# Routed experts of a decoder trunk: the gather of an expert's rows in three steps, and the return of the rows half an expert later

## The chip, the cores and the metric

The kernel runs on one core of a Trainium2 chip. The metric is the device time of one execution in microseconds (us). A core has a matrix engine (PE, with its weight loads, PEld, beside it), a vector engine (DVE), a scalar engine (ACT), GpSimd (POOL) and SyncE (SP), each with a queue of its own that it works off in order; in this kernel SP issues all transfers (DMAs) from memory.

## The reference, cut to what matters

Two decoder layers on 256 tokens of width 1024. The second layer's channel mixer, which the change touches, sends each token through two of eight experts. An expert is a SwiGLU with a hidden width of 3584, so its weights are three matrices of 1024 x 3584 in 32-bit floats, 44 MB for one expert.

```python
def moe_swiglu(x, w_router, w_gate, w_up, w_down):
    ...
    logits = (xf @ w_router).astype(jnp.float32)
    top_logit, top_e = lax.top_k(logits, TOP_K)
    gate = jax.nn.softmax(top_logit, axis=-1)
    ...
        return swiglu(xb, w_gate[e], w_up[e], w_down[e])
    ...
    out = jnp.zeros((n_tok, D), jnp.float32).at[tok_buf].add(y.astype(jnp.float32) * g_buf[:, None])

def swiglu(h, wg, wu, wd):
    return (jax.nn.silu(h @ wg) * (h @ wu)) @ wd
```

## The kernel before, in words

**Split numbers.** Every 32-bit operand is split in two parts of a shorter format, `hi` and `lo`: ACT copies the tile to `hi` with rounding, DVE subtracts to get `lo` (`split`, line 117). A product is then two or three matmuls that add up in one bank of PSUM, the matrix engine's output memory.

**Weight tiles.** All experts' weights come in tiles of 128 x 2048 numbers (1024 KB), 42 for one expert: 14 of the gate matrix, 14 of the up matrix, 14 of the down matrix. For each tile SP issues one DMA (line 114), ACT makes `hi` and DVE makes `lo` (both recorded under line 119). `Tiles.next` (line 886) issues loads and splits for two tiles beyond the one that PE is to take (`AHEAD = 2`). In the trace the raw tiles are called `raw` or `xh`, their high parts `hi` or `xl`, their low parts `lo` or `lnp`, by the buffer that each happens to use.

**Even and odd experts.** The experts are put in an order so that those with many tokens stand at even places and those with few at odd places. An even place is a `Many` (up to 128 rows, three matmuls for a product, lines 137 to 139, 12 matmuls of 512 columns for a tile); an odd place is a `Few` (up to 64 rows, whose high and low parts lie side by side as 128 columns, two matmuls for a product, lines 930 and 931, 8 matmuls for a tile, and a small matmul with `pair`, line 949, that adds the two halves). The text says Many and Few for the two kinds, and e0 to e7 for the experts in order.

**Chunks.** An expert is four chunks: 1024, 1024, 1024 and 512 of its 3584 hidden columns. `run_chunks` (line 961) runs them in a software pipeline over all experts: the gate tiles of a chunk, then the transposes (`turn`) of the chunk before, then the up tiles of this chunk, then the down tiles of the chunk before, then `fold`. So an expert's last down tiles come after the gate and up tiles of the next expert's first chunk.

**Into and out of an expert.** `gather` (line 1154) makes one-hot matrices `oh` of the next expert's slots on DVE (line 1159), multiplies the tokens by them on PE (line 1169, in 32-bit floats), splits the result into that expert's rows, and transposes the one-hots to `ohT` (PE line 1176, DVE copy line 1178). All of it stands in the program ahead of the gate tiles of an expert's third chunk (`before` of chunk 2), for the next expert. At the end of the last chunk's down tiles, `finish` (line 1280) takes the sums: `take` splits them into `yh` and `yl`; then `give` returns the rows to the tokens' order with `ohT` on PE (line 1277, 4 matmuls for one block of 128 tokens) and adds them, weighted, to the running output `f` on DVE (line 1278, 2 instructions for one block); both blocks for e0 to e6, one block for e7.

**What sets the order.** A scheduler at build time gives each engine's queue its order, from the order of the program and from what it reckons to be ready. `tc.issue_after(x)` puts what is inside behind `x` on the engine of `x`, with no wait of its own. `Tiles.paced` (line 894) uses it twice: ACT's instructions inside go behind the `hi` of the last tile made so far, DVE's behind the `lo` of the last but one. Reading the gate sums, the up sums, `turn`, `fold` and `finish` are paced in that way; `gather` is not. In `finish` the return stands, besides, behind the last DVE instruction of `take`.

**PSUM.** Two sets of four banks: `m` (gate and up sums, transposes, gathered rows) and `a` (an expert's two sums of the down product, and the returned rows).

Of the kernel before, what the change touches and what calls it, by code (L numbers as in the profile page):

```python
# [16 lines left out]
DEPTH, T, D, P = 2, 256, 1024, 128  # L17
NB = T // P
# [3 lines left out]
D_FFN, D_EXP, N_EXP, PLE = 2816, 3584, 8, 256  # L22
FEW = 64
# [16 lines left out]
def tile_decoder_trunk(  # L40
# [48 lines left out]
    def mbank(shape, dt=F32):  # L89
        return psum.tile(shape, dt, name="m", tag="m", bufs=4)  # L90
# [26 lines left out]
    def split(hi, lo, src, eng=nc.vector):  # L117

        return nc.scalar.copy(hi, src).ins, eng.tensor_sub(lo, src, hi.bitcast(F32)).ins  # L119
# [46 lines left out]
    for b in range(NB):  # L166
        t = x_tile()
# [13 lines left out]
    before = const.tile([P, P], BF16, name="before", tag="before")  # L181
# [78 lines left out]
    def of_block(xs, b):  # L260
        return tuple(t[:, :, b, :] for t in xs)
# [29 lines left out]
    def load_ln(g, bb, i):  # L291
        t = act.tile([P, 2, D], F32, name="lnp", tag="lnp", bufs=1)
        nc.sync.dma_start(t[:, 0, :], dram(g, i * D, [[0, P], [1, D]]))
        nc.sync.dma_start(t[:, 1, :], dram(bb, i * D, [[0, P], [1, D]]))
        return t
# [531 lines left out]
    class Chunk:  # L827


        def __init__(self, x, ws, c0, n, acc, before=None, after=None):  # L830
            self.x_of, self.ws, self.c0, self.n, self.acc_of = x, ws, c0, n, acc
            self.before, self.after = before, after

        def parts(self, kind):

            if kind < 2:
# [2 lines left out]
                                  self.ws()[2][:, r:r + 256, :].rearrange("o (k p) n -> p (o k) n", p=P))]  # L839
                    for r in range(self.c0, self.c0 + self.n, 256)]  # L840

        def columns(self, kind):

            ps = [mbank([P, 512]) for _ in range(self.n // 512)]
            nk = 2048 // self.n
            for g in range(KD // nk):
                w = self.tiles.next()
                for n, t in enumerate(ps):
                    for k in range(nk):
                        s = slice(self.n * k + 512 * n, self.n * k + 512 * n + 512)  # L850
                        self.mm(t, self.x, nk * g + k, w, s, g + k == 0, nk * g + k == KD - 1)
            return ps

        def gate(self):
            if self.before:
                self.before()
            self.x = self.x_of()
            ps = self.columns(0)
            with self.tiles.paced():
                self.have_gate(ps)  # L860
# [6 lines left out]
        def down(self):  # L867
            acc = self.acc_of()
            for g in range(self.n // 256):
                r = self.c0 + 256 * g  # L870
                w = self.tiles.next()
                for k in range(2):
                    for n in range(2):
                        s = slice(D * k + 512 * n, D * k + 512 * n + 512)
                        self.mm(acc[n], self.ht, 2 * g + k, w, s, r + k == 0, r + 256 == D_EXP and k == 1)
            if self.after:
                with self.tiles.paced():
                    self.after()

    class Tiles:  # L880

# [79 lines left out]
    def run_chunks(chunks, made):  # L961
        parts = []
        for prev, ch in zip([None, *chunks], [*chunks, None]):
            parts += [*(ch.parts(0) + ch.parts(1) if ch else []), *(prev.parts(2) if prev else [])]
        tiles = Tiles(parts, made)
        for prev, ch in zip([None, *chunks], [*chunks, None]):
            if ch:
                ch.tiles = tiles
                ch.gate()
            if prev:  # L970
                with tiles.paced():
                    prev.turn()
            if ch:
                ch.up()
            if prev:
                prev.down()
            if ch:
                with tiles.paced():
                    ch.fold()
# [124 lines left out]
    def moe_ple(i, xt):  # L1104
# [10 lines left out]
        slot = mt([P, NB, N_EXP], "slot")  # L1115
        for b in range(NB):
# [7 lines left out]
            t = mbank([P, N_EXP])  # L1124
# [3 lines left out]
        for b in range(NB):  # L1128
# [12 lines left out]
            t = mbank([P, N_EXP])  # L1141
# [8 lines left out]
        def few(e):  # L1150

            return e % 2 == 1

        def gather(e, slots):

            oh = mt([P, NB, P], "oh", bufs=2)
            n = FEW if few(e) else P
            for b in range(NB):
                phase["picked"] = nc.vector.tensor_scalar(
                    oh[:, b, :].rearrange("p (s n) -> p s n", n=n), slot_i[:, None, :n].to_broadcast([P, P // n, n]),  # L1160
                    slots[:, b, e:e + 1], None, op0=OP.is_equal).ins
            xh, xl = of_block(xe, e % 2)
            ts = [mbank([P, 4, n]) for _ in range(2)]
            for b in range(NB):
                for g, t in enumerate(ts):
                    for k in range(4):

                        c = (4 * g + k) * P
                        nc.tensor.matmul(t[:, k, :], xt[b][:, c:c + P], oh[:, b, :n], start=(b + k == 0),  # L1169
                                         stop=(b == NB - 1 and k == 3))  # L1170
            for g, t in enumerate(ts):
                s = slice(4 * g, 4 * g + 4)
                phase["gathered"] = split(*((xh[:, s, :FEW], xh[:, s, FEW:]) if few(e) else (xh[:, s], xl[:, s])), t)
            t = mbank([P, NB, P])
            for b in range(NB):
                nc.tensor.transpose(t[:, b, :], oh[:, b, :], ident)
            ohT = mt([P, NB, P], "ohT", F32R, bufs=2)
            nc.vector.tensor_copy(ohT, t)
            return xh, xl, ohT


        with tc.issue_after(routed.ins):
            state = {0: gather(0, slot)}
        picked, gathered = phase["picked"], phase["gathered"]
        pp = ple_pre(i, abank, turned)

# [18 lines left out]
        t = mbank([P, N_EXP])  # L1205
# [25 lines left out]
        place = mt([P, N_EXP // 2, 2], "place")  # L1231
# [16 lines left out]
        slots = mt([P, NB, N_EXP], "slots")  # L1248
# [6 lines left out]
        f = []  # L1255
        for b in range(NB):
            t = x_tile()
# [4 lines left out]
        def take(e, acc):  # L1262

            yh, yl, _ = state[e]
            for n in range(2):
                s = slice(4 * n, 4 * n + 4)
                last = split(yh[:, s], yl[:, s], acc[n].rearrange("p (k n) -> p k n", n=P))[1]
            return last

        def give(e, b):  # L1270

            yh, yl, ohT = state[e]
            for n in range(2):
                s = slice(512 * n, 512 * n + 512)
                t = abank([P, 512])
                for k, y in enumerate((yh, yl)):
                    nc.tensor.matmul(t, ohT[:, b, :], y[:, 4 * n:4 * n + 4], start=(k == 0), stop=(k == 1))
                nc.vector.scalar_tensor_tensor(f[b][:, s], t, Gs[:, b, e:e + 1], f[b][:, s], op0=OP.mult, op1=OP.add)

        def finish(e, acc):  # L1280
            with tc.issue_after(take(e, acc)):
                give(e, 0)
                if e < N_EXP - 1:
                    give(e, 1)
                    state.pop(e)

        chunks, cols = [], [(0, 1024), (1024, 1024), (2048, 1024), (3072, 512)]
        for e in range(N_EXP):
            acc, ws = [], []

            def weights(e=e, ws=ws):

                if not ws:
                    if e == 0:
                        k = 0
                        ws.extend(w[0:1] for w in (wg, wu, wd))
                    else:
                        k = nc.values_load(which_i[0:1, e:e + 1], engines=[mybir.EngineType.SP], min_val=0, max_val=N_EXP - 1)
                        ws.extend(w[bass.ds(k, 1)] for w in (wg, wu, wd))
                return ws  # L1300

            def sums(acc=acc):
                if not acc:
                    acc.extend(abank([P, 512]) for _ in range(2))
                return acc

            for c, (c0, n) in enumerate(cols):
                chunks.append((Few if few(e) else Many)(
                    lambda e=e: state[e][0] if few(e) else state[e][:2], weights, c0, n, sums,
                    before=(lambda e=e: state.update({e + 1: gather(e + 1, slots)})) if c == 2 and e + 1 < N_EXP else None,  # L1310
                    after=(lambda e=e, acc=acc: finish(e, acc)) if c == len(cols) - 1 else None))

        made = []
        for g, load in enumerate(chunks[0].parts(0)):
# [6 lines left out]
        phase["hi"] = [x_T("xl", F32R).rearrange("p k b n -> p (k b n)")]  # L1321
        phase["lo"] = [act.tile([P, 2048], F32R, name="lnp", tag="lnp", bufs=1)]
        run_chunks(chunks, made)
        lnp2 = load_ln(ln2_g, ln2_b, i)

        def embed(b, xs, xps, tiles, lnp):
# [64 lines left out]
                for _ in ple[b]:  # L1391
                    pass

        tail(lnp2, lambda: give(N_EXP - 1, 1))


        full = nc.values_load(most_i[0:1, 0:1], min_val=0, max_val=T + P)
        with tc.If(full > P):
            for more in range(2):
                with tc.For_i(0, N_EXP, 1) as e:  # L1400
# [14 lines left out]
                    for g in range(2):  # L1415
                        t = mbank([P, 4, P])
# [104 lines left out]
```

## Time and profile before

| What | Before |
|---|---|
| median of 3 runs | 1484.36 us (1484.25 to 1484.56) |
| the profiled execution's own time | 1485.4 us |
| its span in the trace | 1483.6 us |
| PE, PEld busy | 1418.9 us (96%), 1165.1 us (79%) |
| DVE busy | 1207.4 us (81%) |
| ACT busy | 985.7 us (66%) |
| moved from memory | 436.31 MB, mean 295 GB/s |

The experts run from about 505 to 1445 us of the span. Matmuls overlap in the pipeline and their ends are modelled: a 512-column matmul is shown as some 0.39 us long, while the next one can start 0.23 us after it. So PE's busy share doesn't tell how near it is to its peak; the distance between starts does. The small groups of the profile are cut from its page.

### The profile page before, as it was taken

The numbers are of one execution on the slowest core, as the hardware profiler recorded it, in microseconds if no ns is written. First come the engines' busy times: TensorE is split into PE (matmuls) and PEld (weight loads), VectorE is DVE, ScalarE is ACT, GpSimd is POOL, SyncE is SP. The second block draws the span as 40 slices with busy tenths as digits, with TensorE's granted clock in tenths as the row PEclk, the third lists the DMA queues.
The fourth block names the chain that finished last, engine by engine and source line by source line (L and its number), as shares of the span: only waits on it lengthen the run. The fifth ranks groups of instructions, "written<-read, shape, count | busy, mean of one in ns | idle before, by whom it ended". The sixth has DMA issues, their size and how long they took to land.

```text
span 1483.6 us, 19473 instructions
## 1 busy us (share of the span) xinstructions
PE 1418.9 (96%) x7239; PEld 1165.1 (79%) x7239; DVE 1207.4 (81%) x1393; ACT 985.7 (66%) x1022; POOL 23.3 (2%) x34
## 2 busy tenths in 40 slices
PE   8999999999999999999999999999999999999966
PEld 7987888877987788877778877778887777887745
DVE  6867545467677897889998899988898998889987
ACT  6646433444755776678876777876687886777861
POOL 1000000001000000000000000000000000000000
PEclk9999999999999999999999999999999999999988
DMA  9533555535642499999999999999999999999971
GB/s 296 201 130 121 192 193 175 199 121 165 220 147 110 148 384 334 352 375 380 419 382 340 365 387 374 415 397 341 378 387 358 408 421 364 333 387 373 416 283 59
DMA packets 157382, 438.71 MB, mean 296 GB/s; under 512 B 19744, under 2 KB 41056, under 8 KB 157280
## 3 DMA queue, kind: packets, MB, share of 16 engines
q1 hardware_dynamic: 157280, 437.39, 78.8%
q8 instruction: 59, 0.97, 0.3%
q14 instruction: 43, 0.35, 0.1%
HBM read 436.31 MB, written 1.05 MB: 295 GB/s over the span
## 4 chain that ended last, share of the span: by engine, by line
PE 74%; DVE 13%; DMA 5%; issue 5%; ACT 2%; POOL 0%; SPq 0%; DVEq 0%; ACTq 0%; POOLq 0%
PE m L139 9%; PE m L137 9%; PE m L138 9%; PE a L137 9%; PE a L138 9%; PE a L139 9%; DVE lo L119 7%; PE m L931 4%; PE m L930 4%; DMA raw<-in_moe_w_down_dram 2%; PE m L596 2%; DVE lnp L119 2%; PE m L1169 2%; PE m L949 1%; DMA raw<-in_moe_w_up_dram 1%
## 5 line engine op out<-in xcount | busy, mean ns | idle before, releaser
L119 DVE TENSOR_TENSOR lo<-raw,hi 128x2048 fp32r<-128x2048 f32 (+1 forms) x287 | 640.1, 2256 | 96.5 <-PE m L139 37.7
L119 ACT CAST hi<-raw 128x2048 fp32r<-128x2048 f32 (+1 forms) x289 | 539.6, 1890 | 151.6 <-PE m L138 50.8
L137 PE MATMUL m<-hi,xh 128*128 128x512 f32 x540 | 212.5, 394 | 0.7 <-DVE xl L119 0.7
L139 PE MATMUL m<-lo,xh 128*128 128x512 f32 x540 | 206.8, 392 | 4.6 <-DVE lo L119 4.6
L138 PE MATMUL m<-hi,xl 128*128 128x512 f32 x540 | 210.5, 390 | 0.0
L931 PE MATMUL m<-lo,xh 128*128 128x512 f32 x356 | 136.0, 412 | 10.0 <-DVE lo L119 9.8
L930 PE MATMUL m<-hi,xh 128*128 128x512 f32 x356 | 131.6, 400 | 0.0
L119 DVE TENSOR_TENSOR lnp<-raw,xl 128x2048 fp32r<-128x2048 f32 x56 | 127.9, 2284 | 2.9 <-ACT xl L119 2.8
L139 PEld LDWEIGHTS m<-lo,xh 128*128 128x128 f32 x540 | 101.3, 188 | 26.6 <-DVE lo L119 5.3
L137 PEld LDWEIGHTS m<-hi,xh 128*128 128x128 f32 x540 | 101.4, 188 | 21.4 <-DVE xl L119 0.8
L138 PEld LDWEIGHTS m<-hi,xl 128*128 128x128 f32 x540 | 101.5, 188 | 20.8
L119 ACT CAST xl<-raw 128x2048 fp32r<-128x2048 f32 x56 | 107.3, 1916 | 12.0 <-DMA raw<-in_moe_w_gate_dram 4.0
L137 PE MATMUL a<-hi,hh 128*128 128x512 f32 x272 | 106.8, 395 | 1.6 <-ACT hh L119 1.6
L119 DVE TENSOR_TENSOR lo<-xh,hi 128x2048 fp32r<-128x2048 f32 x45 | 102.8, 2285 | 5.6 <-ACT hi L119 5.1
L138 PE MATMUL a<-hi,hl 128*128 128x512 f32 x272 | 107.0, 393 | 0.0
L139 PE MATMUL a<-lo,hh 128*128 128x512 f32 x272 | 102.5, 395 | 0.0
L931 PEld LDWEIGHTS m<-lo,xh 128*128 128x128 f32 x356 | 68.4, 192 | 30.1 <-DVE lo L119 16.6
L119 ACT CAST hi<-xh 128x2048 fp32r<-128x2048 f32 x45 | 86.3, 1918 | 3.0 <-DMA xh<-in_moe_w_gate_dram 0.9
L930 PEld LDWEIGHTS m<-hi,xh 128*128 128x128 f32 x356 | 68.9, 194 | 13.4
L137 PE MATMUL a<-hi,xh 128*128 128x512 f32 (+1 forms) x168 | 67.2, 406 | 7.1 <-DVE ls L613 3.1
L931 PE MATMUL a<-lo,hh 128*128 128x512 f32 x172 | 65.4, 420 | 6.2 <-DVE lo L119 4.8
L138 PE MATMUL a<-hi,xl 128*128 128x512 f32 (+1 forms) x168 | 67.1, 400 | 1.3 <-DVE xl L119 1.2
(354 smaller groups left out, 2382.5 us busy)
## 6 DMA issues: line engine op xcount, KB each, us to landing
raw<-in_moe_w_gate_dram SPq DMA_DIRECT2D x103, 1024.0 KB, 8.0
raw<-in_moe_w_up_dram SPq DMA_DIRECT2D x95, 1024.0 KB, 8.1
raw<-in_moe_w_down_dram SPq DMA_DIRECT2D x81, 1024.0 KB, 7.6
xh<-in_moe_w_down_dram SPq DMA_DIRECT2D x31, 1024.0 KB, 7.9
xh<-in_moe_w_up_dram SPq DMA_DIRECT2D x17, 1024.0 KB, 8.1
raw<-in_ffn_w_down_dram SPq DMA_DIRECT2D x11, 1024.0 KB, 4.8
raw<-in_w_in_dram SPq DMA_DIRECT2D x10, 1024.0 KB, 6.6
raw<-in_ffn_w_gate_dram SPq DMA_DIRECT2D x10, 1024.0 KB, 5.1
```

The costliest lines, as they stand in the source:

```text
L119: return nc.scalar.copy(hi, src).ins, eng.tensor_sub(lo, src, hi.bitcast(F32)).ins
L137: nc.tensor.matmul(o, lh, rh, start=start, stop=False)
L138: nc.tensor.matmul(o, ll, rh, start=False, stop=False)
L139: nc.tensor.matmul(o, lh, rl, start=False, stop=stop)
L596: nc.tensor.matmul(s[:, a, :], lhsT, rhs, start=True, stop=True)
L930: nc.tensor.matmul(o, x[:, k, :], w[0][:, s], start=start, stop=False)
L931: nc.tensor.matmul(o, x[:, k, :], w[1][:, s], start=False, stop=stop)
L949: nc.tensor.matmul(t[:, j, :], hs[j // 4][:, j % 4 * P:j % 4 * P + P], pair, start=True, stop=True)
L1169: nc.tensor.matmul(t[:, k, :], xt[b][:, c:c + P], oh[:, b, :n], start=(b + k == 0), stop=(b == NB - 1 and k == 3))
```

## The change

`Chunk` no longer has one function before its gate tiles and one after its down tiles. It has a table `hooks` of functions by place: a place is `(kind, g)`, ahead of the g-th tile of the gate (kind 0) or up (kind 1) tiles, or `"end"`, after the down tiles. Each function at a place runs inside `tiles.paced()`.

`gather` is cut in three: `pick` makes the one-hots, `gather` multiplies and splits, `back` transposes the one-hots. In an expert's third chunk they stand ahead of gate tile 0, ahead of gate tile 2, and ahead of up tile 2. `give` is cut in two: `give` has the matmuls and holds the four results in PSUM, `add` has the DVE additions. `take` stays at the end of the last chunk's down tiles; `give` for both blocks stands ahead of gate tile 2 of the next expert's second chunk, and `add` for both ahead of up tile 0 of that chunk. For e7, whose next expert does not exist, `give` and `add` of block 0 follow the last chunk as before, now without `issue_after`, and those of block 1 stay in the tail.

```diff
-        def __init__(self, x, ws, c0, n, acc, before=None, after=None):
+        def __init__(self, x, ws, c0, n, acc, hooks):
...
+        def at(self, place):
+
+            for f in self.hooks.get(place, []):
+                with self.tiles.paced():
+                    f()
+
         def columns(self, kind):
 
             ps = [mbank([P, 512]) for _ in range(self.n // 512)]
             nk = 2048 // self.n
             for g in range(KD // nk):
+                self.at((kind, g))
                 w = self.tiles.next()
...
         def gate(self):
-            if self.before:
-                self.before()
...
-            if self.after:
-                with self.tiles.paced():
-                    self.after()
+            self.at("end")
...
         def give(e, b):
 
             yh, yl, ohT = state[e]
+            ts = []
             for n in range(2):
-                s = slice(512 * n, 512 * n + 512)
                 t = abank([P, 512])
                 for k, y in enumerate((yh, yl)):
                     nc.tensor.matmul(t, ohT[:, b, :], y[:, 4 * n:4 * n + 4], start=(k == 0), stop=(k == 1))
+                ts.append(t)
+            return ts
+
+        def add(e, b, ts):
+            for n, t in enumerate(ts):
+                s = slice(512 * n, 512 * n + 512)
                 nc.vector.scalar_tensor_tensor(f[b][:, s], t, Gs[:, b, e:e + 1], f[b][:, s], op0=OP.mult, op1=OP.add)
-
-        def finish(e, acc):
-            with tc.issue_after(take(e, acc)):
-                give(e, 0)
-                if e < N_EXP - 1:
-                    give(e, 1)
-                    state.pop(e)
...
+            hooks = {
+                (1, (0, 2)): lambda e=e: state.update(given=[give(e - 1, b) for b in range(NB)]) if e else None,
+                (1, (1, 0)): lambda e=e: [add(e - 1, b, ts) for b, ts in enumerate(state["given"])] if e else None,
+                (2, (0, 0)): lambda e=e: state.update({e + 1: [pick(e + 1, slots)]}) if e + 1 < N_EXP else None,
+                (2, (0, 2)): lambda e=e: state[e + 1].extend(gather(e + 1, state[e + 1][0])) if e + 1 < N_EXP else None,
+                (2, (1, 2)): lambda e=e: state[e + 1].append(back(state[e + 1].pop(0))) if e + 1 < N_EXP else None,
+                (len(cols) - 1, "end"): lambda e=e, acc=acc: take(e, acc),
+            }
             for c, (c0, n) in enumerate(cols):
                 chunks.append((Few if few(e) else Many)(
                     lambda e=e: state[e][0] if few(e) else state[e][:2], weights, c0, n, sums,
-                    before=(lambda e=e: state.update({e + 1: gather(e + 1, slots)})) if c == 2 and e + 1 < N_EXP else None,
-                    after=(lambda e=e, acc=acc: finish(e, acc)) if c == len(cols) - 1 else None))
+                    {at: [f] for (place, at), f in hooks.items() if place == c}))
...
         run_chunks(chunks, made)
+        add(N_EXP - 1, 0, give(N_EXP - 1, 0))
```

## Rows read from the trace of the kernel before

**Rows 1.** Stretch: length, busy us of PE, PEld, DVE, ACT, POOL; clock, DMA share, GB/s.

```profile
630.00:650.00 20.00, 20.00 (x105) 16.88 (x104) 15.99 (x10) 18.93 (x16) 0.00 (x0) 1.00 1.03 420
650.00:660.00 10.00, 7.23 (x25) 5.51 (x24) 9.86 (x8) 3.29 (x3) 0.00 (x0) 0.83 0.78 291
660.00:695.00 35.00, 33.71 (x180) 27.83 (x180) 32.42 (x22) 29.14 (x24) 0.00 (x0) 1.00 1.00 368
695.00:730.00 35.00, 34.07 (x156) 25.77 (x156) 34.65 (x18) 30.82 (x22) 0.00 (x0) 1.00 1.03 417
600.00:615.00 15.00, 15.00 (x71) 12.43 (x70) 10.18 (x7) 10.31 (x8) 0.00 (x0) 1.00 0.80 293
795.00:860.00 65.00, 65.00 (x305) 53.65 (x304) 56.51 (x35) 48.10 (x33) 0.00 (x0) 1.00 0.94 353
```

**Rows 2.** Waits in 505:1445: who for whom, us in total, times, longest.

```profile
DVE ohT L1178 <- PE m L1176: 20.7, 4, 5.4
...
DVE x L1278 <- PE a L1277: 16.4, 7, 2.8
```

**Rows 3.** Groups by line in 505:1445: count | busy us, mean ns | idle before.

```profile
L119 DVE TENSOR_TENSOR lo<-raw,hi 128x2048 fp32r<-128x2048 f32 x223 | 502.4, 2284 | 17.2 <-ACT hi L119 17.0
L119 ACT CAST hi<-raw 128x2048 fp32r<-128x2048 f32 x223 | 421.2, 1916 | 50.3 <-DMA raw<-in_moe_w_up_dram 15.8 <-DMA raw<-in_moe_w_gate_dram 13.7 <-DMA raw<-in_moe_w_down_dram 5.1
...
L1278 DVE SCALAR_TENSOR_TENSOR x<-a,Gs,x 128x512 f32<-128x512 f32 x30 | 20.7, 746 | 16.4 <-PE a L1277 16.4
...
L119 ACT CAST xh<-m 128x256 fp32r<-128x256 f32 (+1 forms) x15 | 7.1, 473 | 39.8 <-PE m L1169 39.8
...
L1178 DVE CAST ohT<-m 128x256 fp32r<-128x256 f32 x8 | 3.4, 423 | 21.0 <-PE m L1176 20.7
L1159 DVE TENSOR_SCALAR oh<-slot_i,slots 128x128 f32<-128x128 f32 x14 | 3.3, 276 | 0.0
```

**Rows 4.** DVE's timeline at the step from e0 to e1: start, length, instruction, [idle before].

```profile
646.06 1.28 DVE L119 TENSOR_TENSOR xl<-a,xh 128x512 fp32r<-128x512 f32 x2
650.14 2.75 DVE L1278 SCALAR_TENSOR_TENSOR x<-a,Gs,x 128x512 f32<-128x512 f32 x4 [2.80 <-PE a L1277]
652.80 4.48 DVE L119 TENSOR_TENSOR lo<-raw,hi 128x2048 fp32r<-128x2048 f32 x2
```

**Rows 5.** SP's timeline there: the DMA issues.

```profile
643.97 2.58 SPq L114 DMA_DIRECT2D raw<-in_moe_w_up_dram  x2
655.11 0.37 SPq L114 DMA_DIRECT2D raw<-in_moe_w_down_dram  x1
```

**Rows 6.** PE's timeline there.

```profile
651.30 0.39 PE L930 MATMUL m<-hi,xh 128*128 128x512 f32 x1
651.52 0.39 PE L931 MATMUL m<-lo,xh 128*128 128x512 f32 x1
...
655.14 0.50 PE L931 MATMUL m<-lo,xh 128*128 128x512 f32 x1 [2.77 <-DVE lo L119]
```

**Rows 7.** DVE's timeline at the step from e1 to e2.

```profile
759.51 1.28 DVE L119 TENSOR_TENSOR xl<-a,xh 128x512 fp32r<-128x512 f32 x2
762.53 2.75 DVE L1278 SCALAR_TENSOR_TENSOR x<-a,Gs,x 128x512 f32<-128x512 f32 x4 [1.73 <-PE a L1277]
```

**Rows 8.** PE's timeline there.

```profile
767.53 0.50 PE L139 MATMUL m<-lo,xh 128*128 128x512 f32 x1 [1.53 <-DVE lo L119]
```

**Rows 9.** DVE's timeline around the gather in e1, a Few.

```profile
670.46 0.69 DVE L119 TENSOR_TENSOR xl<-m,xh 128x512 fp32r<-128x512 f32 x1 [0.23 <-ACT xh L119]
672.26 2.29 DVE L119 TENSOR_TENSOR lo<-raw,hi 128x2048 fp32r<-128x2048 f32 x1 [1.11 <-ACT hi L119]
675.03 2.29 DVE L119 TENSOR_TENSOR lnp<-xh,xl 128x2048 fp32r<-128x2048 f32 x1 [0.48 <-ACT xl L119]
```

**Rows 10.** DVE's timeline at a paced transpose in e0, a Many.

```profile
605.79 1.29 DVE L119 TENSOR_TENSOR hl<-m,hh 128x512 fp32r<-128x512 f32 x2 [3.81 <-ACT hh L119]
608.09 2.29 DVE L119 TENSOR_TENSOR lo<-xh,hi 128x2048 fp32r<-128x2048 f32 x1 [1.01 <-ACT hi L119]
```

More of the change, by code (lines that the diff above doesn't have):

```diff
@@ L827, in tile_decoder_trunk @@
     class Chunk:
-        def __init__(self, x, ws, c0, n, acc, before=None, after=None):
+        def __init__(self, x, ws, c0, n, acc, hooks):
             self.x_of, self.ws, self.c0, self.n, self.acc_of = x, ws, c0, n, acc
-            self.before, self.after = before, after
+            self.hooks = hooks
         def parts(self, kind):
@@ L1152, in few, with pick @@
             return e % 2 == 1
-        def gather(e, slots):
+        def pick(e, slots):
             oh = mt([P, NB, P], "oh", bufs=2)
@@ L1161, in gather @@
                     slots[:, b, e:e + 1], None, op0=OP.is_equal).ins
+            return oh
+        def gather(e, oh):
+            n = FEW if few(e) else P
             xh, xl = of_block(xe, e % 2)
@@ L1173, in gather, with back @@
                 phase["gathered"] = split(*((xh[:, s, :FEW], xh[:, s, FEW:]) if few(e) else (xh[:, s], xl[:, s])), t)
+            return xh, xl
+        def back(oh):
             t = mbank([P, NB, P])
@@ L1178, in gather @@
             nc.vector.tensor_copy(ohT, t)
-            return xh, xl, ohT
+            return ohT
         with tc.issue_after(routed.ins):
-            state = {0: gather(0, slot)}
+            oh = pick(0, slot)
+            state = {0: [*gather(0, oh), back(oh)]}
         picked, gathered = phase["picked"], phase["gathered"]
@@ L1392, in tail @@
                     pass
-        tail(lnp2, lambda: give(N_EXP - 1, 1))
+        tail(lnp2, lambda: add(N_EXP - 1, 1, give(N_EXP - 1, 1)))
         full = nc.values_load(most_i[0:1, 0:1], min_val=0, max_val=T + P)
```

## The prediction

> **What bounds the kernel now.** I read the page for the engines' shares, then the waits of the expert stretch, then a table by stretches, and last the timelines at the places that the change touches. The shares alone say little: PE 96%, DVE 81%, DMA full. By stretch it is two regimes. In a Many, PE has work without a break: 65.00 of 65.00 us busy, with the transfers at 353 GB/s, below the 420 that the same queue reaches elsewhere [rows 1]. A tile costs it 12 matmuls whose starts lie 0.23 us apart [rows 6], 2.8 us; DVE needs 2.28 us for the tile's `lo` and ACT 1.92 for its `hi` [rows 3]. In a Few a tile is 8 matmuls, 1.8 us, so DVE and the transfers take over: from 660 to 695 us DVE is busy 32.42 of 35 us while 368 GB/s are moved, and from 695 to 730 it is 34.65 of 35 at 417 GB/s [rows 1]. There each microsecond in which DVE does nothing delays a `lo`, and with it both PE and the raw buffer for which the next DMA waits.
>
> The place to look at is the step from a Many to a Few. `take` ends at 647.3; then DVE waits 2.80 us for PE's return matmuls, adds for 2.75 us, and starts the next `lo` at 652.80 [rows 4]. SP issues nothing from some 646 until 655.11 [rows 5], so only 291 GB/s move from 650 to 660 [rows 1]; PE runs out of tiles and waits 2.77 us [rows 6], after which the clock of that stretch averages 0.83 [rows 1], that is, some 3.4 us of its 10 at the lower level of 1.2 GHz instead of 2.4. At the step from a Few to a Many it is the same in small: DVE waits 1.73 us [rows 7], PE 1.53 us [rows 8]. Over all experts the wait ahead of the additions is 16.4 us in 7 waits [rows 2]: four of 2.8 (Many to Few) and three of 1.7 (Few to Many).
>
> **The change, part by part.**
>
> *The return, cut in two.* The 8 matmuls and 4 additions for one expert stay as they are; no work goes. What goes is the wait between them. The matmuls are now 2 gate tiles behind `take`, 3.7 us of PE in a Few and 5.6 in a Many, so `yl` (ready at 647.3, about 3 us after the last down matmul) is there when PE comes to them. The additions stand 2 tiles behind the matmuls. When DVE reaches them it has just made the `lo` of the first up tile, so PE is at most those few tiles behind; if DVE has to wait there, it is because it is ahead, and PE has tiles in hand.
>
> At the step to a Few (four times) I count the whole 2.80 as gained, 11.2 us. It could be 0, if the transfers bound the Few anyway, or 2.80 and a part of the slow clock. For the whole: from 650 to 695 us, 7.4 us of transfer at 420 GB/s were missed ((129 x 10 + 52 x 35) / 420, [rows 1]), so the queue has room to take up 2.8. Against more: DVE, which stays the limit, is not sped up by PE's clock.
>
> At the step to a Many (three times) PE is the limit, so I count PE's gap and not DVE's: 3 x 1.53 = 4.6 us [rows 8]. Bounds: 0, if a gap opens elsewhere, and 1.73 each.
>
> *The additions at their new place.* 4 x 0.746 [rows 3], merged 2.75 us of DVE, in one block behind `turn`. In a Few, DVE is the limit both at the old place and at the new one: 0. In a Many, the cover is what PE has in hand: with two split tiles, 5.6 us, against 2.75 for the additions and 2.28 for the next `lo`, 5.0. I take 0. With only one tile in hand and the 1.29 of `turn` ahead of them [rows 10], it is 1.29 + 2.75 + 2.28 - 2.8 = 3.5 us each in e2, e4 and e6. What waits behind them is DVE's next `lo`, and for that PE and SP's next DMA.
>
> *The holding of banks.* `given` holds all four `a` banks over two gate tiles and until the additions are done. The next expert's sums need two of them only at its first down tile, four up tiles after the additions: 4 x 1.8 = 7.4 us in a Few against 2.75. Cost 0. The gathered rows now take the two `m` banks that the gate sums leave free. `turn` has to have one back: after the last gather matmul that is a cast and a subtraction, about 1.2 us, against two gate tiles, 3.7 us or more. Cost 0, unless the splits come late; then it falls under the next item.
>
> *The gather.* Same instructions: two one-hots of 0.276 us, the matmuls, four split instructions, one copy of 0.423 us [rows 3]. In a Many the gather makes ACT and DVE wait long now, up to 5.4 us at DVE [rows 2], and PE is not idle for any of it (795 to 860, [rows 1]): nothing to gain; I take 0. In a Few (e1, e3, e5) DVE's waits around it are 0.23, 1.11 and 0.48, 1.8 us [rows 9]. Behind splits and with the one-hots made two tiles earlier they might go, a gain of 5.4 in all; or ACT's cast stands at the head of its queue while PE works off the matmuls between two tiles, and they become longer. The nearest rows are the present waits; I take no change, 0, with both ends kept for the range.
>
> *Queues.* No DMA is added or moved, and SP's order stays; its issues come earlier only because buffers come free earlier. POOL has no part. The end of the program (e7's return and the tail) does the same work as before. The start, e0's own gather, too.
>
> **Sum.** 11.2 + 4.6 = 15.8 us. The profiled execution's own time is 1485.4 (span 1483.6 and 1.8 around it), 1.0 above the median of the runs, 1484.36. So 1469.6 for that execution and 1468.6 for the median.
>
> **The rivals.**
>
> *Bigger: the gather's waits in the Few experts go as well.* 15.8 + 3 x 1.8 = 21.2, so 1463.2. For it: the one-hots no longer share a place with the multiplication, and DVE's part is behind a `lo`. Against: ACT's cast still has to wait for PE's matmuls, and PE now gets them in one place.
>
> *The transfers bound the Few.* From 695 us on they run at 417, which is all that the queue gave anywhere (420 from 630 to 650, [rows 1]); if the earlier start only makes the queue full earlier and PE ends at the same time, the 11.2 goes and 4.6 stays: 1479.8. Against: the 7.4 us missed before 695. The Trainium skill (DMA: Bandwidth & Descriptors, "Where 436 GB/s comes from") puts the ceiling of the core's sixteen ports at 435 GB/s. By that page a Few's 44 MB cannot take less than about 101 us, an estimate from its figure, so such a bound is real; the trace's 420 agrees with it to 4%. What it leaves open is whether a Few has transfers in hand when it starts.
>
> *The waits move along with the additions.* DVE comes to them before PE has done the matmuls, at the limit of the buffers, and stands still as long as before, in the DVE-bound part: 0, so 1484.4. Against: two tiles now lie between matmuls and additions, where none lay before.
>
> *Slower: one tile in hand at the new queue heads.* Each paced block has ACT or DVE standing at the head of its queue until PE has come to the block's matmuls. What follows is fixed: two casts of 0.47, a `hi` of 1.92, a `lo` of 2.28 [rows 3], 5.15 us until PE gets a new tile. The pacing guarantees only one finished `lo` at that point. If it is one, PE loses 5.15 - 2.8 = 2.35 in each of four Many gathers, 5.15 - 1.85 = 3.3 in each of three Few gathers, and 3.5 at the additions of three Many: 9.4 + 9.9 + 10.5 = 29.8, less 15.8: 14.0 slower, 1498.4. It decides from the point where the `lo` of the second tile is queued behind the block instead of ahead of it. Against: the paced transposes in e0 made DVE wait 3.81 and 1.01 us [rows 10] and PE was busy 15.00 of 15.00 us around them [rows 1], so two tiles were in hand there.
>
> **How the numbers follow.** The forecast as summed: 0.53, own range 1463 to 1476 (the clock, and 0.5 to 1 us for each step). The bigger gain: 0.15, down to 1456 if the slow clock's 4 x 1.7 us comes back too. Transfers: 0.12. Waits that move along: 0.08. Slower: 0.12. A measurement of this kernel can tell 0.2%, 3 us, from no change. Faster than 1481.4 are the first three, 0.80; within, 0.08; slower, 0.12. The range 1456 to 1482 leaves the last two out, 0.20.
>
> **What would show it.** Right: no wait of DVE ahead of the additions at either step, or waits there at places where PE has no gap; at the step from e0 to e1 no gap of PE and a clock of 1.00; SP issuing every 2.2 us through that step instead of the hole of some 9 us; and the Few experts' first 45 us at about 375 GB/s instead of 351 ((291 x 10 + 368 x 35) / 45, [rows 1]). The additions stand in the second chunk, with a `lo` right ahead of them and right behind them. Wrong: PE gaps in the Many experts near the gather or behind `turn` (the slower case), the hole at SP moved by some four tiles to the additions' new place (the waits move along), or PE's gaps gone at the steps and new ones of the same size in the 40 us behind them, at 420 GB/s (the transfers).

## The result and the profile after

The changed kernel takes 1467.15 us (median of 4 runs, 1465.99 to 1467.34) against 1484.46 for the kernel before (4 runs beside it): a ratio of 0.9886, 95% interval 0.9872 to 0.9900, 17.3 us less. Forecast were 1468.6 us and a range of 1456 to 1482. The profiled execution took 1467.25 us, its span 1465.4, 18.2 less than the span before (the profiled execution of the kernel before was about 1 us above the median of its runs, so the spans differ by more than the medians).

The first view is the table by stretches of the changed kernel: stretch, length, busy time of PE, PEld, DVE, ACT and POOL with instruction counts, granted clock, DMA share, GB/s. It answers to [rows 1].

```profile
648.00:658.00 10.00, 10.00 (x49) 8.36 (x47) 10.00 (x8) 7.99 (x7) 0.00 (x0) 1.00 1.03 422
658.00:695.00 37.00, 35.17 (x186) 28.20 (x185) 35.03 (x25) 30.22 (x24) 0.00 (x0) 1.00 1.01 394
695.00:730.00 35.00, 34.03 (x155) 25.65 (x154) 34.76 (x18) 30.06 (x22) 0.00 (x0) 1.00 1.02 405
785.00:850.00 65.00, 65.00 (x311) 54.03 (x310) 54.11 (x34) 43.98 (x31) 0.00 (x0) 1.00 0.92 349
```

The ten microseconds at the step from e0 to e1 moved 291 GB/s before and move 422 now; PE is busy for all of them instead of 7.23, and the clock is 1.00 instead of 0.83. The Many stretch (last row) is as it was: PE without a break, at 349 GB/s. PE still has a gap in the Few, of 1.1 us behind the additions, in each of the four:

```profile
662.25 0.50 PE L934 MATMUL m<-lo,xh 128*128 128x512 f32 x1 [1.12 <-DVE lo L119]
```


DVE's timeline of the changed kernel at that step (start, length, instruction, [idle before]); line 1297 is the addition, 1278 before. It answers to [rows 4].

```profile
645.75 1.28 DVE L119 TENSOR_TENSOR xl<-a,xh 128x512 fp32r<-128x512 f32 x2
647.27 4.49 DVE L119 TENSOR_TENSOR lo<-raw,hi 128x2048 fp32r<-128x2048 f32 x2 [0.24 <-ACT hi L119]
651.68 2.29 DVE L119 TENSOR_TENSOR lo<-xh,hi 128x2048 fp32r<-128x2048 f32 x1
653.88 0.68 DVE L960 TENSOR_TENSOR hl<-hl,m 128x512 f32<-128x512 f32 x1
654.48 0.74 DVE L1297 SCALAR_TENSOR_TENSOR x<-a,Gs,x 128x512 f32<-128x512 f32 x1
655.14 2.28 DVE L119 TENSOR_TENSOR lnp<-raw,xl 128x2048 fp32r<-128x2048 f32 x1
657.34 0.68 DVE L119 TENSOR_TENSOR hh<-hl,hh 128x512 fp32r<-128x512 f32 x1
657.94 2.06 DVE L1297 SCALAR_TENSOR_TENSOR x<-a,Gs,x 128x512 f32<-128x512 f32 x3
659.92 8.88 DVE L119 TENSOR_TENSOR lo<-raw,hi 128x2048 fp32r<-128x2048 f32 x4
```

Behind the split of the sums (`xl<-a`) the next `lo` follows after 0.24 us, where 2.80 us of waiting and 2.75 of additions stood. The additions come three tiles later, one ahead of a `lo` and three behind it, and wait for nothing. A second wait has gone with the first. Before, PE came so late out of the hole that ACT stood 6.71 us ahead of its copies of the sums (line 937), and DVE had to wait for the `hi` behind them (ACT's and DVE's timelines of the kernel before):

```profile
659.67 0.59 ACT L937 COPY w<-m 128x512 f32<-128x512 f32 x1 [6.71 <-PE m L931]
662.93 2.29 DVE L119 TENSOR_TENSOR lo<-raw,hi 128x2048 fp32r<-128x2048 f32 x1 [0.65 <-ACT hi L119]
```

That wait of DVE was 0.65 us in e1, 0.60 in e3, 0.51 in e5 and 0.44 in e7; ACT's wait in e1 is 1.92 now. Over all experts the group of the additions says the same: its idle time was 16.4 us [rows 3] and is now

```profile
L1297 DVE SCALAR_TENSOR_TENSOR x<-a,Gs,x 128x512 f32<-128x512 f32 x32 | 22.5, 742 | 0.0
```

SP's timeline there, the answer to [rows 5]. The hole from 646 to 655 us is one from 646 to 649.6, and a smaller one follows: of the next issues one comes at 657.45 and the one behind it at 662.23, beside PE's gap.

```profile
643.65 2.58 SPq L114 DMA_DIRECT2D raw<-in_moe_w_up_dram  x2
649.59 2.57 SPq L114 DMA_DIRECT2D raw<-in_moe_w_down_dram  x2
```

The step from e1 to e2 on DVE, the answer to [rows 7]: the `lo` follows the split at once, and the additions wait for nothing.

```profile
755.75 1.28 DVE L119 TENSOR_TENSOR xl<-a,xh 128x512 fp32r<-128x512 f32 x2
756.95 2.28 DVE L119 TENSOR_TENSOR lo<-raw,hi 128x2048 fp32r<-128x2048 f32 x1
...
763.55 1.40 DVE L1297 SCALAR_TENSOR_TENSOR x<-a,Gs,x 128x512 f32<-128x512 f32 x2
```

Both kernels issue the same 336 weight transfers in the same order, so the issue of the same tile in both traces can be subtracted. That gives where the time comes from, step by step (issue after less issue before, in us, each read a little behind the step):

| | before the first step | e0 to e1 | e1 to e2 | e2 to e3 | e3 to e4 | e4 to e5 | e5 to e6 | e6 to e7, with e7 |
|---|---|---|---|---|---|---|---|---|
| lies earlier by | 0.3 | 3.7 | 5.6 | 8.9 | 10.7 | 13.5 | 15.3 | 19.3 |
| this step | | 3.4 | 1.9 | 3.3 | 1.8 | 2.8 | 1.8 | 4.0 |

Four steps from a Many to a Few give 13.5 us, three from a Few to a Many 5.5. The last two transfers lie only 18.3 earlier, and with them the end.

The length of an expert on DVE, from one split of the sums to the next, shows the same without the end. For e1, before and after (columns as in the table by stretches):

```profile
646.06:759.51 113.45, 107.81 (x510) 86.11 (x510) 105.14 (x64) 91.37 (x67) 0.00 (x0) 0.98 1.00 391
645.75:755.75 110.00, 106.56 (x510) 84.63 (x510) 104.77 (x65) 91.11 (x67) 0.00 (x0) 1.00 1.02 406
```

DVE does the same work in 3.45 us less. The other three Few experts are shorter by 3.30, 2.88 and 3.07, 12.7 in all, and the three Many that follow a Few by 1.83, 1.76 and 1.75, 5.3 in all.

### The profile page after: what moved, and what is told of

Its sections match the earlier page's. It is cut to its first block, busy times and chain, and to the rows that moved or that the text cites. A ratio compares the mean times of both kernels' runs of the same rounds, so it can differ in the third digit from the quotient of the medians.

```text
span 1465.4 us, 19472 instructions
## 1 busy us (share of the span) xinstructions
PE 1413.5 (96%) x7239; PEld 1161.0 (79%) x7239; DVE 1206.4 (82%) x1393; ACT 984.4 (67%) x1022; POOL 21.1 (1%) x34
## 4 chain that ended last, share of the span: by engine, by line
PE 69%; DVE 15%; issue 6%; DMA 5%; ACT 3%; SPq 1%; POOL 0%; DVEq 0%; ACTq 0%; POOLq 0%
PE a L137 9%; PE a L138 9%; PE a L139 9%; DVE lo L119 9%; PE m L137 8%; PE m L139 8%; PE m L138 8%; PE m L934 3%; PE m L933 3%; DVE lnp L119 2%; DMA raw<-in_moe_w_gate_dram 2%; DMA raw<-in_moe_w_up_dram 2%; PE m L596 2%; PE m L1177 2%; ACT hi L119 1%
## 5 line engine op out<-in xcount | busy, mean ns | idle before, releaser
L139 PE MATMUL m<-lo,xh 128*128 128x512 f32 x540 | 206.1, 391 | 0.0
L934 PE MATMUL m<-lo,xh 128*128 128x512 f32 x356 | 133.3, 403 | 5.3 <-DVE lo L119 5.1
L119 ACT CAST xl<-raw 128x2048 fp32r<-128x2048 f32 x56 | 107.3, 1916 | 12.7 <-DMA raw<-in_moe_w_gate_dram 6.3
L137 PE MATMUL a<-hi,hh 128*128 128x512 f32 x272 | 106.7, 395 | 1.6 <-ACT hh L119 1.6
L933 PE MATMUL a<-hi,hh 128*128 128x512 f32 x172 | 62.4, 402 | 6.2 <-DVE hh L119 6.2
```

The lines of the kernel that those rows point to most:

```text
L137: nc.tensor.matmul(o, lh, rh, start=start, stop=False)
L139: nc.tensor.matmul(o, lh, rl, start=False, stop=stop)
L933: nc.tensor.matmul(o, x[:, k, :], w[0][:, s], start=start, stop=False)
L934: nc.tensor.matmul(o, x[:, k, :], w[1][:, s], start=False, stop=stop)
```

## The experiments

All are compared by their ratio to runs of the kernel before on the same chip; those runs spread over 1480 to 1488 us there, so ratios say more than medians. The changed kernel itself ran only beside the four runs of the first section, so where an experiment is compared with it, two ratios from different sets of runs are compared.

**return_only: the return of the change, the gather of before.**

```diff
-                (2, (0, 0)): ... pick(e + 1, slots) ...
-                (2, (0, 2)): ... gather(e + 1, state[e + 1][0]) ...
-                (2, (1, 2)): ... back(state[e + 1].pop(0)) ...
+                (2, "start"): lambda e=e: whole(e + 1) if e + 1 < N_EXP else None,   # all three, ahead of the chunk, unpaced
```

> The return of the rows as in the changed kernel (matmuls ahead of gate tile 2, additions ahead of up tile 0 of the next expert's second chunk); the gather whole and unpaced ahead of the third chunk, as in the kernel before. Theory A, the gain is DVE's wait ahead of the additions that is gone (16.4 us in 7 waits before): 1467 to 1470 us, nearly all of the 17.3 us gained. Theory B, the gather cut in three carries a part, as DVE's waits around it in the Few experts (1.8 us each in three) go: some 5 us less gained, 1472 to 1474 us. Theory C, the order of the queues as a whole (pacing) makes the gain: more than half lost, over 1476 us.

Measured 1467.69 us, ratio 0.9883 (0.9856 to 0.9911): all of the gain.

**gather_only: the gather of the change, the return of before.**

```diff
-                (1, (0, 2)): ... give(e - 1, b) ...
-                (1, (1, 0)): ... add(e - 1, b, ts) ...
-                (len(cols) - 1, "end"): lambda e=e, acc=acc: take(e, acc),
+                (len(cols) - 1, "end"): lambda e=e, acc=acc: finish(e, acc),
```

> The gather in three paced places as in the changed kernel; the return as in the kernel before, right behind the split of the expert's sums. Theory A: no change, 1482 to 1486 us, with the 7 waits ahead of the additions still at 16 us in all. Theory B: 4 to 6 us faster, 1478 to 1480 us. Theory C: more than half of the gain, under 1476 us.

Measured 1484.24 us, ratio 0.9997 (0.9984 to 1.0011): nothing. The wait ahead of the additions is the old one (who for whom, us in total, times, longest, in 505 to 1445 us):

```profile
DVE x L1297 <- PE a L1290: 16.3, 7, 2.8
```

Theory A holds in both halves. Why the gather's new places give nothing is to be seen in DVE's timeline of this kernel around the gather in e1:

```profile
686.46 0.69 DVE L119 TENSOR_TENSOR xl<-m,xh 128x512 fp32r<-128x512 f32 x1 [0.20 <-ACT xh L119]
688.27 2.29 DVE L119 TENSOR_TENSOR lo<-xh,hi 128x2048 fp32r<-128x2048 f32 x1 [1.12 <-ACT hi L119]
691.25 0.69 DVE L960 TENSOR_TENSOR hl<-hl,m 128x512 f32<-128x512 f32 x1 [0.69 <-PE m L952]
```

0.20, 1.12 and 0.69 us in place of 0.23, 1.11 and 0.48 [rows 9]: the gather has moved, and its waits with it; the third, 0.69, now stands ahead of `turn`'s product (line 960).

**no_distance: the additions directly behind their matmuls, in the second chunk.**

```diff
-                (1, (0, 2)): lambda e=e: state.update(given=[give(e - 1, b) for b in range(NB)]) if e else None,
-                (1, (1, 0)): lambda e=e: [add(e - 1, b, ts) for b, ts in enumerate(state["given"])] if e else None,
+                (1, (0, 2)): lambda e=e: [add(e - 1, b, give(e - 1, b)) for b in range(NB)] if e else None,
```

> The changed kernel with the additions directly behind their matmuls, both ahead of gate tile 2 of the next expert's second chunk: the return still lies two gate tiles behind the split of the sums, but nothing lies between matmuls and additions. If what pays is that the return has left the place right behind the split (theory A1): DVE's waits ahead of the additions stay under 1 us each in the Few experts, 1466 to 1471 us. If what pays is the distance between matmuls and additions (theory A2): the waits come back at the new place, 2 to 3 us each in four Few experts, and some 8 to 12 us of the gain go, 1475 to 1480 us.

Measured 1473.18 us, ratio 0.9925 (0.9897 to 0.9952), between the two ranges. The waits at the additions are short, as A1 has it, but there are seven:

```profile
DVE x L1297 <- PE a L1290: 5.8, 7, 1.0
```

Against the changed kernel 5.8 us are lost too ((0.9925 - 0.9886) x 1484.5; the two intervals overlap by 0.0003). So most of the gain comes from leaving the place behind the split, and the distance between matmuls and additions is worth about the waits that come back without it. That the two sums are equal is in part chance: from split to split a Few is 1.0 to 2.3 us longer than in the changed kernel, for a wait of 0.95, and a Many 0.3, for a wait of 0.66. Neither theory as I had put it.

**unpaced: the hooks at their places, not queued behind splits.**

```diff
             for f in self.hooks.get(place, []):
-                with self.tiles.paced():
-                    f()
+                if place == "end":
+                    with self.tiles.paced():
+                        f()
+                else:
+                    f()
```

> The changed kernel with all hooks at the same places, but only the split of the sums at an expert's end paced; the five other hooks stand in the program there without being queued behind splits. Theory A: the places do it, within 3 us of the changed kernel, 1464 to 1470 us. Theory C, the pacing does it: ACT and DVE again take up the gather's and the return's instructions early and wait for PE at the queue's head, with gaps of PE at each of the seven steps, 1474 us or more.

Measured 1470.61 us, ratio 0.9908 (0.9882 to 0.9933). That is 0.6 above theory A's range and well under theory C's 1474: the places make most of the gain. Its interval overlaps that of the changed kernel; whether the pacing adds the 3.3 us between the two, ((0.9908 - 0.9886) x 1484.5), these runs don't settle. The first additions of this kernel stand two tiles earlier on DVE than in the changed kernel and the waits ahead of them are 5.7 us in 7 times, as in no_distance.

**late_adds: only the additions moved, the matmuls of the return where they were.**

```diff
-                (1, (0, 2)): ... give(e - 1, b) ...
-                (len(cols) - 1, "end"): lambda e=e, acc=acc: take(e, acc),
+                (len(cols) - 1, "end"): lambda e=e, acc=acc: leave(e, acc),   # take, and give for both blocks behind it
```

> The changed kernel with the return's matmuls back where they were before, behind the split of the sums at the expert's end; only the additions stay ahead of up tile 0 of the next expert's second chunk. Theory A (what paid is that DVE no longer stands ahead of the additions while tiles wait for their lo): nearly all of the gain stays, 1466 to 1471 us, and DVE waits under 1 us in all ahead of the additions. Rival (the matmuls' place counts too: PE waits for the split sums at the steps): 3 us or more of the gain go, 1471 us or more, with PE gaps ahead of the return's matmuls.

Measured 1466.26 us, ratio 0.9887 (0.9865 to 0.9910): all of the gain, with 0.2 us of PE waiting ahead of the return's matmuls and no wait of DVE ahead of the additions. Together with gather_only this leaves the place of the four DVE instructions of each expert as what counts of the whole change.

**thin_adds: what the additions cost at the new place.**

```diff
         def add(e, b, ts):
+            w = 16 if e < N_EXP - 1 else 512
             for n, t in enumerate(ts):
-                s = slice(512 * n, 512 * n + 512)
+                s, t = slice(512 * n, 512 * n + w), t[:, :w]
```

> The changed kernel with the additions of e0 to e6 on 16 of their 512 columns (the other columns of the returned rows are left out of the sum). An addition then takes some 0.15 us instead of 0.746, 2.4 us less of DVE in each expert. If DVE still is the limit of a Few: 2.4 us in each of the four returns that lie in a Few, nothing in the three in a Many: 7 to 10 us faster than the changed kernel, 1457 to 1460 us. If the transfers are the limit there (they now run at 394 GB/s from 658 to 695 us, some 3 us missed in a Few): 4 to 7 us, 1460 to 1463 us. If the additions are hidden at their new place: within 2 us of the changed kernel.

Measured 1459.45 us, ratio 0.9839 (0.9816 to 0.9861), 7.0 us below the changed kernel by the ratios. The group has a mean of 289 ns over 28 thin and 4 full additions; with 0.742 for the full ones a thin one is 0.22 us, so 2.1 us went from each expert, not 2.4. By the subtracted transfers the steps to a Few gain 1.7 us more than in the changed kernel in e1, e3 and e5 and 1.0 more in e7, and the step from e1 to e2 nothing more (1.9 in both). So DVE's work is on the path in a Few, four fifths of it in the first three, and hidden in a Many. The 7.0 us lie where the expected ranges of DVE and of the transfers as the limit meet; what takes the last fifth was not followed up.

**adds_spread: two pairs of additions, two tiles apart.**

```diff
-                (1, (1, 0)): lambda e=e: [add(e - 1, b, ts) for b, ts in enumerate(state["given"])] if e else None,
+                (1, (1, 0)): lambda e=e: add(e - 1, 0, state["given"][0]) if e else None,
+                (1, (1, 2)): lambda e=e: add(e - 1, 1, state["given"][1]) if e else None,
```

> The changed kernel with the additions in two pairs, block 0 ahead of up tile 0 and block 1 ahead of up tile 2, instead of four in one place. If the gap of 1.27 us that PE still has behind the additions in each Few (four times) is on the path: 2 to 4 us faster than the changed kernel, 1463 to 1465 us. If DVE's sum of work is the limit there and not how it is spread (theory A): within 1.5 us of the changed kernel, and the gaps come in two halves.

Measured 1466.12 us, ratio 0.9884 (0.9864 to 0.9903): no change, as theory A has it. The gap of PE behind the additions was put at 1.27 us in what was expected; that one lies in e7, well behind the step, and those behind the additions are 1.12 and 1.11. In e1 the 1.12 became two gaps of 0.75 and 0.73.

**gather_apart: the gather's splits two tiles behind its matmuls.**

```diff
-                (2, (0, 0)): ... pick(e + 1, slots) ...
-                (2, (0, 2)): ... gather(e + 1, state[e + 1][0]) ...
+                (1, (1, 2)): ... pick(e + 1, slots) ...
+                (2, (0, 0)): ... gather(e + 1, state[e + 1][0]) ...           # the matmuls alone
+                (2, (0, 2)): ... parted(e + 1, state["rows"]) ...             # their splits
                 (2, (1, 2)): ... back(state[e + 1].pop(0)) ...
```

> The changed kernel with the one-hots ahead of up tile 2 of the second chunk, the gather's matmuls ahead of gate tile 0 of the third chunk and its splits ahead of gate tile 2, two tiles behind the matmuls, as the return has it. DVE's waits around the gather in the three Few experts that have one (0.16 and 1.11 us and, at the transposes behind, 0.69) should go. If DVE's waits count there as they did at the return: 3 to 6 us faster than the changed kernel, 1461 to 1464 us. If the transfers, at 404 to 421 GB/s around that place, are the limit by then: within 1.5 us.

Measured 1459.61 us, ratio 0.9844 (0.9824 to 0.9864): faster than both kernels, 6.2 us below the changed one by the ratios, a little more than the 3 to 6 expected. DVE's timeline around the gather in e1 has no wait left:

```profile
678.84 2.28 DVE L119 TENSOR_TENSOR lnp<-raw,xl 128x2048 fp32r<-128x2048 f32 x1
681.04 1.27 DVE L119 TENSOR_TENSOR xl<-m,xh 128x512 fp32r<-128x512 f32 x2
682.24 2.27 DVE L119 TENSOR_TENSOR lo<-xh,hi 128x2048 fp32r<-128x2048 f32 x1
684.58 0.69 DVE L960 TENSOR_TENSOR hl<-hl,m 128x512 f32<-128x512 f32 x1
```

and its stretches show DVE busy 36.93 of 37 us, and the transfers at full rate after 695:

```profile
658.00:695.00 37.00, 35.65 (x186) 29.22 (x185) 36.93 (x25) 31.53 (x25) 0.00 (x0) 1.00 1.01 398
695.00:730.00 35.00, 34.18 (x157) 26.47 (x158) 33.90 (x18) 29.88 (x21) 0.00 (x0) 1.00 1.03 418
```

By the subtracted transfers it is 2.1 us in each of e1, e3 and e5, and nothing in e7, which has no gather: about the sum of the three waits that were left (0.16, 1.11 and 0.69, 1.96). Over the whole of e1 that is 107.91 us for the 110.00 of the changed kernel, with DVE's work as it was and the transfers at 411 GB/s:

```profile
644.46:752.37 107.91, 105.09 (x510) 84.98 (x510) 104.60 (x65) 91.23 (x67) 0.00 (x0) 1.00 1.02 411
```

**apart_alone: that gather with the return of before.**

```diff
 (gather_apart, and)
-                (1, (0, 2)): ... give(e - 1, b) ...
-                (1, (1, 0)): ... add(e - 1, b, ts) ...
-                (len(cols) - 1, "end"): lambda e=e, acc=acc: take(e, acc),
+                (len(cols) - 1, "end"): lambda e=e, acc=acc: finish(e, acc),
```

> The gather as in the kernel gather_apart (one-hots, matmuls and splits at three places two tiles or more apart), the return as in the kernel before. If the two gains are of the same kind and add up: gather_apart was 6 to 7 us faster than the changed kernel, so 1477 to 1479 us here. If the gather's gain needs the return's (a limit, the transfers or DVE, that comes free only when the hole at the step is gone): 1481 us or more.

Measured 1480.2 us, ratio 0.9969 (0.9958 to 0.9980): 4.6 us faster, between the two ranges as given; its interval reaches to 6.2. From split to split e1, e3 and e5 are 1.5, 1.4 and 1.5 us shorter than in the kernel before, where gather_apart made them 2.1, 2.1 and 2.0 shorter than the changed kernel. So most of the gather's gain comes without the return's; in the traces about 0.6 us in each of the three Few comes only with it.

**apart_pool: the additions of a Few's return on ACT and POOL.**

```diff
+                if not few(e):
+                    for c, tag in ((0, "pth"), (256, "ptl")):
+                        w, o = ph((P, 2, P), tag, bufs=2), f[b][:, 512 * n + c:512 * n + c + 256]
+                        w = w.rearrange("p k n -> p (k n)")
+                        nc.scalar.activation(w, t[:, c:c + 256], AF.Copy, scale=Gs[:, b, e:e + 1])
+                        nc.gpsimd.tensor_tensor(o, o, w, op=OP.add)
+                    continue
```

> gather_apart, and for the four experts whose rows return in a Few the additions are taken off DVE: ACT copies each quarter of the returned rows to memory weighted (256 columns, some 0.4 us, 8 for one expert, 3.1 us), POOL adds it to the running output. 2.75 us of DVE go from each Few; the run with thin additions gained some 7 us over the changed kernel from 2.4 us less in each expert. If DVE is the limit in a Few and ACT (31.5 us busy of 37 there) can take 3.1 us more: 3 to 7 us faster than gather_apart, 1453 to 1457 us. If ACT becomes the limit, or POOL's additions slow DVE's: no gain or a loss, 1459 to 1465 us.

Measured 1478.46 us, ratio 0.9958 (0.9942 to 0.9974): the worse case, and far worse than I had it, 17 us above gather_apart. ACT's timeline in e1 shows where it starts (the copies are line 1304, POOL's additions 1305):

```profile
655.87 1.27 ACT L940 COPY w<-m 128x512 f32<-128x512 f32 x2 [1.92 <-PE m L934]
657.03 0.62 ACT L119 CAST hh<-hl 128x512 fp32r<-128x512 f32 x1
657.55 0.48 ACT L1304 ACTIVATE pth<-a,Gs 128x256 f32<-128x256 f32 x1
...
661.33 0.47 ACT L1304 ACTIVATE ptl<-a,Gs 128x256 f32<-128x256 f32 x1 [0.22 <-POOL x L1305]
661.70 7.29 ACT L119 CAST hi<-raw 128x2048 fp32r<-128x2048 f32 x4
```

and DVE's what it does:

```profile
657.96 0.69 DVE L119 TENSOR_TENSOR hh<-hl,hh 128x512 fp32r<-128x512 f32 x1
663.62 4.78 DVE L119 TENSOR_TENSOR lo<-raw,hi 128x2048 fp32r<-128x2048 f32 x2 [4.97 <-ACT hi L119]
```

The eight copies stand in one block, 4.2 us, right where ACT has just waited for PE (1.92), so no `hi` is made from 654 to 661.7; DVE saves 2.75 us of additions and waits 4.97. From the sixth copy on ACT also waits for POOL, 0.21 to 0.22 us each time. Over the whole of e1 it comes to 4.1 us more than in gather_apart:

```profile
647.06:759.04 111.98, 106.80 (x510) 86.01 (x510) 102.25 (x60) 93.96 (x75) 5.94 (x8) 0.98 1.00 398
```

DVE is idle for 9.73 of these 111.98 us, where it was idle for 3.31 of 107.91: 6.4 us more of waiting for 2.4 less of work. e3 is 5.8 us longer than in gather_apart, e5 4.0. ACT's spare time in a Few is real, but not at that place. The same copies spread over several tiles were not tried.

## Why the prediction was right

**The main term: the wait ahead of the additions.** Right in mechanism and nearly in size. The step to a Few was put at 2.80 each, 11.2; it gave 3.4, 3.3, 2.8 and 4.0, 13.5 by the transfers, of which 1.0 is lost again in the last two, and 12.7 from split to split. The sum had left out DVE's second wait behind the hole, 0.65, 0.60, 0.51 and 0.44 us, 2.2 in all; against it 0.2 us of waiting remain ahead of the first `lo` at each step. These two terms bring the sum to about 12.5. The slow clock (0.83 in that stretch, now 1.00) had been left out because DVE sets the pace; no run takes it apart, but little is left for it. The step to a Many was put at PE's gap, 1.53; it gave 1.9, 1.8 and 1.8, 5.5 for 4.6, a little over DVE's wait of 1.73 that I had as the upper bound. Why it follows DVE's wait and not PE's gap was not looked into.

**The place of the return.** The reason given was that two gate tiles now lie between `take` and the matmuls and two between these and the additions. The first part is not needed (late_adds); what is needed is that DVE gets to its next `lo` first, and that more than one tile of DVE's work lies ahead of the additions (no_distance, with one tile, loses 5.8 us). They do not stand in one block, as I had it, but as one and three in e1 and as two and two in e2.

**The additions at the new place: 0.** Right for both kinds. In a Few they are still on the path (thin_adds), where they were on it before; in a Many they are hidden. PE's gap of 1.1 us behind them in each Few was not foreseen, nor SP's pause beside it; I had written that PE would have no gap at the step and that SP would issue every 2.2 us. The gap costs nothing by itself, since DVE's sum of work sets the pace there (adds_spread).

**The gather: 0.** Right, and shown alone (gather_only). The three waits of a Few's gather are about as long as they were, 1.96 us for 1.82. The bigger rival put 5.4 us on these waits; the change doesn't take them away, but gather_apart does, and gains 6.2. So that rival was wrong about the change and nearly right about the price.

**The rivals.** The transfers do not bind at the step: the stretch that moved 291 and 368 GB/s moves 422 and 394 now, (422 x 10 + 394 x 37) / 47 = 400 over the first 47 us, where I had forecast 375. What is still missed to 420 in these 47 us is 2.2 us, so that bound is near now, and gather_apart, with 411 GB/s over the whole of e1, is nearer. The Trainium skill (DMA: Bandwidth & Descriptors, "Where 436 GB/s comes from") puts the ceiling of the ports at 435 GB/s; the 422 here lie 3% below it. Waits that move along: refuted by the group with 0.0 idle. One tile in hand: refuted by the Many stretch, 65.00 of 65.00 us busy.

## What to carry to other kernels

When an engine that works off its queue in order sets the pace, look in its timeline for a result that goes to another engine and comes straight back, as the split sums do here by way of PE: the instruction that takes it back costs the same anywhere in the stretch, but the wait ahead of it goes when other work of that queue is put first. Here one tile of such work left waits of 0.66 to 0.95 us, and three tiles left none; moving a block as a whole (the gather) moved its waits with it and gave nothing. And a wait costs about its length only where nobody behind it has work in hand: waits of DVE of up to 5.4 us in a Many stand beside a PE without a gap, while 2.0 us in a Few cost 2.1.

## What the runs showed of the hardware

Handing the additions to an idle engine is dear in its own way. In apart_pool POOL takes some 0.73 us for 256 columns (1.13 for the first), and ACT's weighted copy of 256 columns out of PSUM 0.48 us, so a block that takes DVE 2.75 us takes ACT 4.2, waits for POOL included, and POOL about 6 (eight times 0.73). Transfers at 422 GB/s beside DVE and PE that are busy for 10.00 of 10 us are no slower than the 420 of a stretch in which DVE is busy for 16 of 20 us [rows 1]. DVE keeps its pace while TensorE's clock is low: before, from 655 to 661 us, the clock averages 0.72, and the `lo` that starts at 657.20 takes 2.28 us, as at 1.00.
